# A trunk layer's input projection: 4096 of its columns by Strassen's seven products, with transposed gates applied late

## The chip, the cores and the metric

One Trainium2 chip; the kernel is one launch on one of its cores. The metric is the device time of that launch in microseconds, lower is better. Of three runs the median is 2184.79 us (2183.13 to 2187.67). A core has five engines that work beside each other and wait for one another through semaphores: TensorE (PE; matrix multiplication, with its weight loads shown as PEld), VectorE (DVE), ScalarE (ACT), GpSimd (POOL) and SyncE (SP, which here only issues DMAs).

## The reference

One layer of a hybrid decoder: 1024 rows of 2048 values. One projection of the normalized input gives 7184 columns, which feed three mixers side by side; their output is normalized per head, gated, projected back and added to the input. Then the rows attend to 256 memory rows, and a final norm follows.

```python
h = rmsnorm(x, norm_mix[l])
(sb_q, sb_k, sb_v, sb_g,                     # stick-breaking attention: 4 x 1024 columns, 8 heads of 128
 gla_q, gla_k, gla_v, gla_r, gla_g,          # gated linear attention (GLA): 256, 256, 512, 16, 512
 sgu_u, sgu_v, sgu_g) = jnp.split(h @ w_in[l], IN_OFFSETS, axis=-1)   # spatial gating (SGU): 3 x 512
o_sb = from_heads(stick_breaking_attention(sb_q, sb_k, sb_v))
o_gla = from_heads(gla_chunked(gla_q, gla_k, gla_v, log_alpha))
o_sgu = chunked_sgu(jax.nn.gelu(sgu_u), jax.nn.gelu(sgu_v), sgu_norm[l], w_sgu[l], b_sgu[l])
mix = jnp.concatenate([o_sb, o_gla, o_sgu], axis=-1)
mix = rmsnorm(mix.reshape(B, S, N_MIX_HEADS, HEAD_DIM), out_norm[l]...).reshape(B, S, MIX_WIDTH)
gate = jax.nn.silu(jnp.concatenate([sb_g, gla_g, sgu_g], axis=-1))
x = x + (mix * gate) @ w_out[l]
x = x + memory_cross_attention(rmsnorm(x, norm_xattn[l]), rmsnorm(mem, norm_mem[l]), w_xq[l], w_xkv[l], w_xo[l])
return rmsnorm(x, final_norm)
```

## The kernel before, in words

**Arithmetic.** Each float32 operand of a large product is held as two float32r tiles that add up to it: `split_to` (L142) casts on ACT and subtracts on DVE. A product is three matmuls (`mm3`, L184): high x low, high x high, low x high. The normalized and transposed input `hT` lies in SBUF as sixteen such pairs of [128, 512] pieces for each half of the rows.

**Stages.** After the norm and the first columns of v (to about 115 us), `natural` (L269) computes blocks of 512 columns with rows on partitions: the rest of v, GLA's v, SGU's u and v, and the gates of SGU and GLA with their SiLU (to about 630 us); they go to scratch in DRAM. After the keys and values of the memory (to 700 us) comes the stretch that the change rewrites: `weave` (L224) runs a list of groups, each a weight load (`raw_weights`, a DMA by SP; `split_to`) and four *steps*. `column_block` (L195) is 128 columns in sixteen steps of six 128x512 matmuls, the columns on partitions. Between the steps stand *tasks*, each with a time counted in steps: SGU (a task `sgu_out` writes its result), then GLA in two pairs of heads, then the eight heads of attention. So projection matmuls fill the time in which the tasks wait for ACT and DVE. The gates of attention (`block_g`) lie beside SGU and GLA, k and q of head h+1 (`block_k`, `block_q`) beside head h; a head has 32 steps.

**GLA.** A pair of heads runs seven *levels* (a chunk of 128 rows, halved again and again). A level forms decay factors `d` (L653), scaled queries `ql` (L663) and keys (`d<-d,k`, L666) on DVE, multiplies them on PE (`z<-ql,d`) and copies the wanted blocks into `attn` under a mask (COPY_PREDICATED, L677). Its output `og` and SGU's `y` are multiplied by their gates on POOL (L749, L543) and go to `mix_scr`, transposed.

**Attention.** `attend` (L835): `scores` makes a tile of scores on PE, three activations, a DVE step (L861), a mask multiply on the diagonal (L863), a scan from the right (L865), a subtraction (L871) and an activation (L872). `turn`, 5.3 steps later, transposes two of those on PE and splits the result into `aTh` and `aTl`; `values` multiplies with v into the PSUM bank `av`, of which there is one. At the end of a quarter of the rows `square` copies the output out of PSUM (`oc`, L903) and squares it on ACT; `close`, 2.5 steps later, sums the squares with two matmuls by `ones_r` into the other half of the same bank, takes ln and exp on ACT (L914, L915) and multiplies `oc` (L917).

**Output projection.** `mixed` (L956) loads 128 columns of the mix for half of the rows and splits them; for k < 8 (attention) it also loads the gate, takes its SiLU and multiplies on POOL (L970). The order is k = 8 to 15 first.

**What sets the order.** PE runs the woven part in program order (`keep_in_program_order`, L172 to L182). The other engines' orders come from a scheduler that sees the dependences and the buffers. Each engine takes its instructions in order, so one that waits holds up all behind it. Buffers limit what can run ahead: three raw weight tiles (`wr`), three split ones (`wh`, `wl`), four PSUM banks for projections (`pj`), two for scores (`z`), one for transposes (`tr`), one `av`.

```python
def split_to(hi, lo, src, eng=dve):
    act.copy(hi, src)
    eng.tensor_tensor(out=lo, in0=src, in1=f32(hi), op=ALU.subtract)
...
UNIT, LAG_T, STEP_T, LAG_V, LAG_S, AHEAD = 32 / 12, 5.3, 2, 2, 2.5, 4
```

## Time and profile before

| | value |
|---|---|
| median of three runs | 2184.79 us (2183.13 to 2187.67) |
| the profiled execution: its own time, the span of the profile | 2184.6 us |
| PE, PEld busy | 2125.8 us (97%), 1767.4 us (81%) |
| DVE, ACT, POOL busy | 1020.7 (47%), 860.9 (39%), 163.5 us (7%) |
| matmul records | 10525 |
| DMA | 231.18 MB, 106 GB/s on average |

The profile gives each engine's busy time; a view by stretches gives it for a window of the span, with the instruction count in brackets; a view by groups gives, for each line, engine, operation and shape, the count, the busy time, the mean of one in ns, the idle time of the engine just ahead of them and what ended it. The order in time lists start, duration and instruction. A line number is that of the kernel before unless said otherwise.

### The profile page before, as it was taken

To read this page: it belongs to the slowest core of one execution; us is meant where nothing else is said; L and a number is where in the kernel's file an instruction comes from. 1 tells how busy PE (TensorE), PEld (TensorE's weight loads), DVE (VectorE), ACT (ScalarE), POOL (GpSimd) and SP (SyncE) were. 2 spreads that over 40 slices of the span, in tenths; PEclk is the share of its full clock that TensorE was granted. 3 is DMA by queue.
4 is the path that set the end of the run, shared out by engine and by line. 5 is a ranking of instruction groups with operands and counts; after the bars stand their busy time and mean duration, and the time that the engine had idled before them with its cause. 6 is when DMAs were issued, how large, how long until landed. Compare 5 with 4: busy or idle time off the path is not lost.

```text
span 2184.6 us, 28465 instructions
## 1 busy us (share of the span) xinstructions
PE 2125.8 (97%) x10525; PEld 1767.4 (81%) x10525; DVE 1020.7 (47%) x1984; ACT 860.9 (39%) x1987; POOL 163.5 (7%) x273
## 2 busy tenths in 40 slices
PE   6999999999999999999999999999989999999997
PEld 6998888888887767878888888888877878888885
DVE  6621211111115627375377677776753121377674
ACT  6421111221215424242356565666654121356552
POOL 2110000000000110101111111111012000000001
PEclk9999999999999999999999999999999999999999
DMA  7541321331317621313222222222267231655632
GB/s 215 151 146 49 126 87 49 97 97 49 98 55 219 184 61 44 107 34 92 78 57 55 56 63 56 61 54 56 83 192 231 69 124 49 207 201 154 216 121 92
DMA packets 181847, 231.18 MB, mean 106 GB/s; under 512 B 17270, under 2 KB 106956, under 8 KB 179532
## 3 DMA queue, kind: packets, MB, share of 16 engines
q1 hardware_dynamic: 170572, 214.68, 32.1%
q0 software_dynamic: 11136, 14.69, 2.6%
q8 instruction: 83, 1.36, 0.3%
q14 instruction: 56, 0.46, 0.1%
HBM read 177.93 MB, written 51.38 MB: 105 GB/s over the span
## 4 chain that ended last, share of the span: by engine, by line
PE 44%; DVE 8%; ACT 5%; issue 4%; DMA 2%; POOL 1%; DVEq 0%; SPq 0%; POOLq 0%; ACTq 0%
PE pj L175 31%; PE z L175 6%; PE av L175 4%; PE tr L180 1%; DVE a L865 1%; DVE a L871 1%; PE tr L175 1%; ACT a L872 1%; DMA mraw<-mix 1%; ACT t L859 1%; ACT t L860 1%; DVE t L861 1%; DVE ql L663 1%; ACT t L858 1%; DVE wl L144 1%
## 5 line engine op out<-in xcount | busy, mean ns | idle before, releaser
L144 DVE TENSOR_TENSOR wl<-wr,wh 128x512 fp32r<-128x512 f32 (+1 forms) x392 | 267.6, 683 | 773.8 <-ACT wh L143 767.6
L175 PE MATMUL pj<-slot,wh 128*128 128x512 f32 x2048 | 576.9, 398 | 1.6 <-DVE qT L144 1.6
L143 ACT CAST wh<-wr 128x512 fp32r<-128x512 f32 (+1 forms) x395 | 237.6, 602 | 798.4 <-PE av L175 548.6
L175 PE MATMUL pj<-wh,slot 128*128 128x512 f32 (+1 forms) x1760 | 500.7, 370 | 0.0
L175 PEld LDWEIGHTS pj<-slot,wh 128*128 128x128 f32 x2048 | 369.7, 188 | 72.4 <-issue 2.3
L175 PEld LDWEIGHTS pj<-wh,slot 128*128 128x128 f32 x1760 | 321.5, 190 | 54.8
L175 PE MATMUL pj<-wl,slot 128*128 128x512 f32 (+1 forms) x880 | 328.9, 374 | 1.7 <-DVE wl L144 1.5
L175 PE MATMUL pj<-slot,wl 128*128 128x512 f32 x1024 | 327.9, 391 | 0.0
L175 PEld LDWEIGHTS pj<-slot,wl 128*128 128x128 f32 x1024 | 192.2, 188 | 42.7
L175 PEld LDWEIGHTS pj<-wl,slot 128*128 128x128 f32 x880 | 167.1, 190 | 30.3 <-DVE wl L144 2.3
L175 PE MATMUL z<-wh,slot 128*128 128x512 f32 x576 | 178.6, 390 | 0.7 <-DVE slot L144 0.7
L175 PEld LDWEIGHTS z<-wh,slot 128*128 128x128 f32 x576 | 108.2, 188 | 24.1 <-DVE slot L144 1.9
L175 PE MATMUL z<-wl,slot 128*128 128x512 f32 x288 | 112.5, 391 | 4.4 <-DVE xo L982 2.7
L861 DVE SCALAR_TENSOR_TENSOR t<-z,t 128x384 f32<-128x384 f32 (+2 forms) x96 | 53.4, 556 | 94.3 <-ACT t L860 94.2
L872 ACT ACTIVATE a<-a 128x384 f32<-128x384 f32 (+2 forms) x96 | 50.4, 525 | 114.5 <-DVE a L871 114.4
L175 PE MATMUL pj<-slot,oT 128*128 128x512 f32 x384 | 92.7, 396 | 0.0
L175 PE MATMUL tr<-wh,slot 128*128 128x512 f32 x288 | 88.7, 389 | 0.0
L175 PE MATMUL av<-wh,slot 128*128 128x512 f32 x288 | 88.7, 389 | 0.0
L175 PEld LDWEIGHTS pj<-slot,oT 128*128 128x128 f32 x384 | 71.0, 188 | 15.7
L175 PE MATMUL z<-kT,qT 128*128 128x512 f32 (+3 forms) x288 | 71.1, 355 | 0.0
L175 PEld LDWEIGHTS z<-wl,slot 128*128 128x128 f32 x288 | 54.0, 188 | 17.2 <-DVE xo L982 3.6
L144 DVE TENSOR_TENSOR aTl<-tr,aTh 128x512 fp32r<-128x512 f32 (+2 forms) x112 | 55.2, 493 | 19.3 <-ACT aTh L143 18.2
(252 smaller groups left out, 2684.2 us busy)
## 6 DMA issues: line engine op xcount, KB each, us to landing
wr<-in_w_in_dram SPq DMA_DIRECT2D x216, 256.0 KB, 2.8
wr<-in_w_out_dram SPq DMA_DIRECT2D x88, 256.0 KB, 2.8
xt<-in_x_dram SPq DMA_DIRECT2D x32, 256.0 KB, 4.8
wr<-in_w_xkv_dram SPq DMA_DIRECT2D x32, 256.0 KB, 3.2
v<-v_scr POOLq DMA_DIRECT2D x64, 128.0 KB, 2.8
xr<-in_x_dram SPq DMA_DIRECT2D x32, 256.0 KB, 5.1
x<-xo SPq DMA_DIRECT2D x32, 256.0 KB, 4.4
x2t<-x SPq DMA_DIRECT2D x8, 1024.0 KB, 7.2
```

Of the source, the lines that this page charges most:

```text
L143: act.copy(hi, src)
L144: eng.tensor_tensor(out=lo, in0=src, in1=f32(hi), op=ALU.subtract)
L175: i = pe.matmul(o, l, r, start=start, stop=stop)
L180: i = pe.transpose(o, i_, ident)
L663: dve.tensor_tensor(out=gl["ql"][r_, :, hh, :].rearrange("p c (b i) -> p c b i", i=h), in0=gl["q"][r_, :].rearrange("p (c b i) -> p c b i" ...
L858: act.activation(tw, z, AF.Abs)
L859: act.activation(tw, tw, AF.Exp, scale=-1.0)
L860: act.activation(tw, tw, AF.Ln, bias=1.0)
L861: dve.scalar_tensor_tensor(out=tw, in0=z, scalar=0.0, in1=tw, op0=ALU.max, op1=ALU.add)
L865: dve.tensor_tensor_scan(out=aw[:, ::-1], data0=tw[:, ::-1], data1=tw[:, ::-1], initial=init, op0=ALU.add, op1=ALU.max)
L871: dve.tensor_tensor(out=aw, in0=z, in1=aw, op=ALU.subtract)
L872: act.activation(aw, aw, AF.Exp)
```

## The change

**Seven products for eight.** Two blocks of 128 columns, two halves of the 2048 input values and two halves of the 1024 rows make a 2x2 by 2x2 product of blocks. Strassen's scheme replaces its eight block products by seven, on sums and differences of the blocks; four sums of products then give the result. This is done for 4096 columns: q and k of attention (a pair is a head's q and k), its gate, and the gates of GLA and SGU, which were `natural` blocks. Sixteen pairs, in two passes over all of them:

- The **first pass** computes products 1, 7 and 6 beside SGU and GLA: per pair eight *units* of nine matmuls, which count as 1.5 steps. Per unit two DMAs load a raw tile of [128, 512] with the four weight blocks, POOL adds two overlapping parts of it (`combine_first`, 384 elements a partition), and the sum is split. `evac_first` copies product 1 on ACT, adds it to the two others on DVE and writes both to DRAM (`part_scr`).
- The **second pass** computes products 5, 2, 3 and 4 beside attention: units of twelve matmuls, which count as 2; the POOL subtraction (`combine_second`, 2 x 128 elements) works in place. `evac_second` copies two products on ACT, subtracts on POOL from the two parts read back, and has four DVE additions from PSUM; the results go to DRAM: q and k to `qk_scr`, gates to `g_scr`. For four of the pairs (gates of GLA and SGU) it also takes the SiLU there: exp, ln, exp on ACT and a POOL multiply for each of four tiles, in buffers `se` of the raw weights' pool.

**The sums of the input.** `sums_round`, eight times, adds the two parts of four pieces of `hT` on POOL, forms five sums on DVE and writes seven tiles to DRAM; `place` reads them back for each pass and splits them (56 in all). The GLA q and k blocks move ahead of everything (steps 0 to 64), their results to DRAM; the first pass is steps 64 to 256, the second 256 to 512.

**What follows.** Attention reads q and k back from DRAM and splits them (`load_k`, `load_q`); a head has 30.3 steps. The mask multiply on DVE becomes an `affine_select` on POOL. `square` only squares; `close` sums with one float32 matmul, and its last DVE operation reads the output from PSUM. SGU and GLA no longer apply their gates; `mixed` does for k >= 8, with two loads into the raw weights' pool and a POOL multiply. `actp` has twelve buffers and a second pool `more` four, `wr` four. On PE 128x512 matmuls become 384 fewer and the two of `close` one; with no rows merged, SP's order has 1441 rows for 811, POOL's 669 instructions for 273, DVE's 2145 for 1986, ACT's 2026 for 1781.

```diff
-        def square(o, sh):
-            sq = sb.tile([P, 256], F32, tag="sq", name="sq")
-            t = sb.tile([P, 2, 256], F32R, tag="sh", name="sh")
-            oc = sb.tile([P, 256], F32, tag="oc", name="oc")
-            dve.tensor_copy(oc, o[0][:, :256])
             act.activation(sq, o[0][:, :256], AF.Square)
-            dve.tensor_copy(t[:, 0, :], sq)
-            dve.tensor_tensor(out=t[:, 1, :], in0=sq, in1=f32(t[:, 0, :]), op=ALU.subtract)
-            sh += [sq, t, oc]
+            sh.append(sq)
 
         def close(p, o, sh):
-            sq, t, oc = sh
-            st = o[0][:, 256:]
-            for i in range(2):
-                mm(st, ones_r, t[:, i, :], i == 0, i == 1)
+            sq, st = sh[0], o[0][:, 256:]
+            mm(st, ones_f, sq, True, True)
             act.activation(sq, st, AF.Ln, scale=1.0 / P, bias=eps_t[:, 0:1])
             act.activation(sq, sq, AF.Exp, scale=-0.5)
-            on = sb.tile([P, 256], F32, tag="on", name="on")
-            dve.scalar_tensor_tensor(out=on, in0=oc, scalar=col("out", h), in1=sq, op0=ALU.mult, op1=ALU.mult)
-            sp.dma_start(on_scr[h][:, p * 256:p * 256 + 256], on)
+            dve.scalar_tensor_tensor(out=sq, in0=o[0][:, :256], scalar=col("out", h), in1=sq, op0=ALU.mult, op1=ALU.mult)
+            sp.dma_start(on_scr[h][:, p * 256:p * 256 + 256], sq)
...
+    AHEAD_RAW = 2
+    def quarters(pairs, joint=0):
+        raw, tw = {}, {}
+        units = [[(pair, k, banks) for k in range(8)] for pair in pairs for banks in ({},)]
...
+        def load(j):
+            for i in range(0 if not j else j + AHEAD_RAW, min(j + AHEAD_RAW + 1, len(units))):
+                fetch(i)
+            pair, k, _ = units[j]
...
+            t, n = pair["combine"](raw.pop(j))
+            hi = whl.tile([P, 512], F32R, tag="wh", name="wh")
+            lo = whl.tile([P, 512], F32R, tag="wl", name="wl")
+            split_to(hi[:, :n], lo[:, :n], t[:, :n])
...
+            for i, c in pair["products"]:
+                th, tl = cut((hi, lo), c * P, c * P + P)
+                sh, sl = pair["sums"].at(i, k)
+                mm(banks[i], th, sh, k == 0, False)
+                mm(banks[i], th, sl, False, False)
+                mm(banks[i], tl, sh, False, k == 7)
...
+    def combine_first(raw):
+        t = bp.tile([P, 3 * P], F32, tag="ts", name="ts")
+        pool.tensor_tensor(out=t, in0=raw[:, :3 * P], in1=raw[:, P:], op=ALU.add)
+        return t, 3 * P
+
+    def combine_second(raw):
+        r3 = raw.rearrange("p (b n) -> p b n", n=P)
+        pool.tensor_tensor(out=r3[:, 0:4:3], in0=r3[:, 0:4:3], in1=r3[:, 2:0:-1], op=ALU.subtract)
+        return raw, 4 * P
...
+            act.copy(c12, banks[5])
+            act.copy(c21, banks[2])
+            pool.tensor_tensor(out=c11, in0=c11, in1=c12, op=ALU.subtract)
+            pool.tensor_tensor(out=c22, in0=c22, in1=c21, op=ALU.subtract)
+            dve.tensor_tensor(out=c12, in0=banks[3], in1=c12, op=ALU.add)
...
+            for t, b, half in ((c12, 1, 0), (c22, 1, 1), (c21, 0, 1), (c11, 0, 0)):
+                if silu:
+                    e = wraw.tile([P, 512], F32, tag="wr", name="se")
+                    act.activation(e, t, AF.Exp, scale=-1.0)
+                    act.activation(e, e, AF.Ln, bias=1.0)
+                    act.activation(e, e, AF.Exp, scale=-1.0)
+                    pool.tensor_tensor(out=t, in0=t, in1=e, op=ALU.mult)
...
         if k >= 8:
-            t = wraw.tile([P, 512], F32, tag="wr", name="mraw")
+            t, g_ = (wraw.tile([P, 512], F32, tag="wr", name=nm) for nm in ("mraw", "graw"))
             sp.dma_start(t, mix_scr[k - 8][:, sl])
+            sp.dma_start(g_, g_scr[k][:, sl])
+            pool.tensor_tensor(out=t, in0=t, in1=g_, op=ALU.mult)
```

How the change moves instructions is shown at three places. The first is PE at the end of a quarter in the attention, before (`av<-sh,ones_r` is the sum of squares, `av<-aTl,v` the next quarter's first values, `pj` the projection):

```order
L175 MATMUL pj<-slot,wh 128x512 x4
L175 MATMUL pj<-slot,wl 128x512 x2
L175 MATMUL av<-sh,ones_r 128x256 x2
L175 MATMUL pj<-slot,wh 128x512 x4
L175 MATMUL pj<-slot,wl 128x512 x2
L175 MATMUL av<-aTl,v 128x256
L175 MATMUL av<-aTh,v 128x256 x2
```

The same place of the change (`av<-sq,ones_f` is the sum of squares):

```order
L207 MATMUL pj<-slot,wh 128x512 x2
L207 MATMUL pj<-slot,wl 128x512
L207 MATMUL av<-sq,ones_f 128x256
L207 MATMUL av<-aTl,v 128x256
L207 MATMUL av<-aTh,v 128x256 x2
L207 MATMUL av<-aTl,v 128x256
L207 MATMUL av<-aTh,v 128x256 x2
L212 MATMUL tr<-ident,a 128x128 x3
```

The six projection matmuls between the sum and the next values are gone from this place. Of the 32 sums, 17 stand directly ahead of values now, seven have twelve matmuls between, and the last of each head has more.

The second place is DVE in the levels of GLA (`wl` is a split of projection weights; `d`, `ql`, `attn` are the level's), before:

```order
L677 COPY_PREDICATED attn<-masks,z 128x8x64 x2
L663 TENSOR_TENSOR ql<-q,d 64x8x64 x2
L653 TENSOR_TENSOR d<-bc 128x1024
L666 TENSOR_TENSOR d<-d,k 128x1024
L677 COPY_PREDICATED attn<-masks,z 128x16x32 x2
L663 TENSOR_TENSOR ql<-q,d 64x8x64 x2
L144 TENSOR_TENSOR wl<-wr,wh 128x512
L666 TENSOR_TENSOR d<-d,k 128x1024
L653 TENSOR_TENSOR d<-bc 128x1024
L677 COPY_PREDICATED attn<-masks,z 128x32x16 x2
```

And of the change (`ts` is what POOL has added):

```order
L877 COPY_PREDICATED attn<-masks,z 128x8x64 x2
L863 TENSOR_TENSOR ql<-q,d 64x8x64 x2
L853 TENSOR_TENSOR d<-bc 128x1024
L866 TENSOR_TENSOR d<-d,k 128x1024
L176 TENSOR_TENSOR wl<-ts,wh 128x384 x2
L877 COPY_PREDICATED attn<-masks,z 128x16x32 x2
L863 TENSOR_TENSOR ql<-q,d 64x8x64 x2
L853 TENSOR_TENSOR d<-bc 128x1024
L866 TENSOR_TENSOR d<-d,k 128x1024
L176 TENSOR_TENSOR wl<-ts,wh 128x384 x2
```

Two splits of 384 stand in each level, each behind a POOL addition, where about one split of 512 stood in every second level.

The third is SP where the output projection starts (`mraw` is a tile of the mix, `graw` of the gate, `wr` a weight), before:

```order
L963 DMA mraw<-mix_161 128x512
L154 DMA wr<-in_w_out_dram 128x512
L963 DMA mraw<-mix_162 128x512
L154 DMA wr<-in_w_out_dram 128x512
L918 DMA on_152<-on 128x256
L963 DMA mraw<-mix_163 128x512
L154 DMA wr<-in_w_out_dram 128x512
```

And of the change:

```order
L186 DMA wr<-in_w_out_dram 128x512 x2
L1157 DMA mraw<-mix_263 128x512
L1158 DMA graw<-g_146 128x512
L1157 DMA mraw<-mix_264 128x512
L1158 DMA graw<-g_147 128x512
L1110 DMA on_137<-sq 128x256
L186 DMA wr<-in_w_out_dram 128x512
L1157 DMA mraw<-mix_265 128x512
L1158 DMA graw<-g_148 128x512
L186 DMA wr<-in_w_out_dram 128x512
```

A tile takes two loads in place of one, and both come from the pool of four buffers that the weights use too; a buffer comes free when POOL has multiplied (gate) or the split has read it (mix).

More of the change, by code (lines that the diff above doesn't have):

```diff
@@ L229, in weave @@
         groups[0][0]()
-        for j, (_, steps) in enumerate(groups):
+        for j, (_, steps, *w) in enumerate(groups):
             if j + 1 < len(groups):
@@ new lines, in trunk, with place, stage_load @@
+    summed = {}
+    sB, sA = Sums(), Sums()
+    def place(sums, i, r, pool=actp):
+        if r % 4 == 0:
+            sums.t[i, r // 4] = (slot(pool=pool), slot(pool=pool))
+        hi, lo = (t[:, r % 4, :] for t in sums.t[i, r // 4])
+        split_to(hi, lo, summed.pop((i, r)))
+    def stage_load(i, r, pool):
+        t = pool.tile([P, 512], F32, tag="st", name="st", bufs=6 if pool is cq else 10)
+        sp.dma_start(t, sum_scr[i, r])
+        summed[i, r] = t
+    pr0, pr1 = gla_blocks(0, range(4)), gla_blocks(1, (0, 2, 1, 3))
@@ new lines, in trunk, with to_cq @@
+    groups += pr0[0] + pr0[1] + [g for both in zip(*pr1) for g in both]
+    def to_cq():
+        kv.close()
+        bp.open()
+        cq_open()
+    later(3.2, to_cq)
+    for m in range(2):
+        later(2 + m, mem_keys, m)
+    for j in range(8):
+        later(5 + j, gla_rank, j // 4, 4 * (j % 4))
+    for r in range(8):
+        later(8 + 4.5 * r, sums_round, r)
+    for n, (r, i) in enumerate([(r, i) for r in range(8) for i in (1, 7, 6)]):
+        t = 48.2 + 0.7 * n if n < 12 else 64.2 + 0.8 * (n - 12)
+        later(max(46, t - 4), stage_load, i, r, cq)
+        later(t, place, sB, i, r)
@@ L512, in sgu_load @@
+    groups += quarters([first(n) for n in range(16)], 2)
+    later(UB + 0.01, more.close)
+    sta = Stage("sta", 10, "right")
     def sgu_load(s):
-        t = {nm: sg.tile([P, 512], F32, tag=f"in{nm}", name=nm) for nm in ("sv", "su", "sg")}
-        for nm in ("sv", "su", "sg"):
+        t = {nm: sg.tile([P, 512], F32, tag=f"in{nm}", name=nm) for nm in ("sv", "su")}
+        for nm in ("sv", "su"):
             sp.dma_start(t[nm], nat_scr[nm][s])
@@ L797, in trunk @@
+    for n, (i, r) in enumerate(late):
+        later(UA + 0.1 + 0.6 * (n - 6), stage_load, i, r, sta)
+        later(UA + 0.2 + 0.6 * n, place, sA, i, r)
+    groups += quarters([second(n) for n in range(16)])
     sb = Stage("sb")
     kTs, qTs = {}, {}
-    consts = {}
     def sb_open():
         sb.open()
-        before = sb.tile([P, P], F32, name="before")
-        pool.affine_select(out=before, in_=ones_f, pattern=[[-1, P]], compare_op=ALU.is_gt, fill=0.0,
-                           base=0, channel_multiplier=1)
-        consts["before"] = before
@@ L1116, in load_wxo @@
         if n == 0:
-            wxo[k] = [(slot(), slot())]
+            wxo[k] = [tuple(slot(pool=actp if k else more) for _ in range(2))]
         h, l = wxo[k][0]
@@ L1193, in trunk @@
     xa.close()
+    more.close()
     if dbg is not None:
```

322 lines of the change are left out of this document (207 added, 115 removed).

## The prediction

> **What bounds the kernel now.** First the page: the busy time of each engine, then the span in forty slices (digits are tenths of a slice).
>
> ```profile
> span 2184.6 us, 28465 instructions
> ...
> PE 2125.8 (97%) x10525; PEld 1767.4 (81%) x10525; DVE 1020.7 (47%) x1984; ACT 860.9 (39%) x1987; POOL 163.5 (7%) x273
> ...
> PE   6999999999999999999999999999989999999997
> ...
> DVE  6621211111115627375377677776753121377674
> ACT  6421111221215424242356565666654121356552
> ...
> PEclk9999999999999999999999999999999999999999
> ```
>
> TensorE is busy for 97% of the span, at full clock in every slice, and falls under nine tenths only at both ends and in slice 31. Of 2184.6 us it is idle for 58.8. So matmuls that go away shorten the span, as long as the other engines can follow. They are near half load on average, but not evenly: the next view gives the busy time of each engine, with the instruction count, in the stretches that the change touches (columns: stretch, its length, PE, PEld, DVE, ACT, POOL, granted clock, DMA share, GB/s).
>
> ```profile
> 300.00:600.00 300.00, 300.00 (x1326) 248.47 (x1325) 39.35 (x60) 57.95 (x95) 0.00 (x0) 1.00 0.27 82
> 700.00:800.00 100.00, 97.62 (x476) 75.73 (x476) 50.61 (x140) 35.70 (x138) 21.04 (x30) 1.00 0.52 148
> 900.00:1000.00 100.00, 96.00 (x483) 78.43 (x483) 65.91 (x98) 38.66 (x71) 8.69 (x7) 1.00 0.21 62
> 926.00:978.00 52.00, 51.06 (x249) 40.97 (x248) 35.34 (x47) 23.57 (x31) 1.97 (x1) 1.00 0.15 41
> 1110.00:1550.00 440.00, 436.67 (x2275) 365.17 (x2274) 310.20 (x602) 269.96 (x607) 51.74 (x134) 1.00 0.23 59
> 1600.00:1700.00 100.00, 93.49 (x400) 74.00 (x400) 40.84 (x58) 44.71 (x83) 21.22 (x16) 1.00 0.70 226
> ```
>
> The stretch 300 to 600 is pure projection: 300.0/1326 = 0.2262 us for a 128x512 matmul. In 700 to 800 (spatial gating) PE loses 2.4%, around the GLA levels (900 to 1000) 4.0%, in seven heads of attention (1110 to 1550, 62.9 us a head) 0.8%, where the output projection starts (1600 to 1700) 6.5%.
>
> **The change part by part.** The sum is made against the profiled execution, 2184.6 us, which is 0.2 below the median of the runs.
>
> *Matmuls.* 4096 columns took 3072 matmuls; 16 pairs x 8 units x 7 products x 3 take 2688. 384 x 0.2262 = **-86.9 us**. At the end of each quarter of a head one f32 matmul takes the place of two f32r ones (32 times); each f32 matmul leaves two records.
>
> ```profile
> L175 PE MATMUL av<-sh,ones_r 128*128 128x256 f32 x64 | 13.6, 289 | 1.9 <-DVE sh L905 1.3 <-DVE sh L906 0.5
> L175 PE MATMUL av<-state,q 128*128 128x256 f32 x28 | 8.3, 378 | 0.0
> L175 PE MATMUL z<-ql,d 128*128 128x128 f32 x224 | 28.2, 279 | 7.2 <-DVE d L666 6.9
> ```
>
> The old pair costs 13.6/32 = 0.425 us, an f32 matmul of this size 8.3/14 = 0.59: +5.4. PE's own term is **-81.5 us**.
>
> *What the other engines get.* Each of 256 units now has an addition on POOL ahead of its split (ACT cast, DVE subtract).
>
> ```profile
> L144 DVE TENSOR_TENSOR wl<-wr,wh 128x512 fp32r<-128x512 f32 x360 | 254.1, 706 | 746.4 <-ACT wh L143 740.2 <-DMA xr<-in_x_dram 4.8 <-PE tr L180 0.6
> L143 ACT CAST wh<-wr 128x512 fp32r<-128x512 f32 x363 | 224.6, 619 | 766.9 <-PE av L175 548.6 <-PE pj L175 185.3 <-DMA wr<-in_w_xkv_dram 9.5
> L970 POOL TENSOR_TENSOR mraw<-mraw,graw 128x512 f32<-128x512 f32 x16 | 21.2, 1326 | 57.0 <-ACT graw L969 57.0
> L749 POOL TENSOR_TENSOR og<-og,gg 128x256 f32<-128x256 f32 x16 | 13.4, 841 | 102.8 <-ACT v L748 102.8
> L871 DVE TENSOR_TENSOR a<-z,a 128x384 f32<-128x384 f32 x16 | 8.8, 552 | 2.3 <-POOL carry L869 2.3
> ```
>
> The second pass's POOL addition is of 256 elements a partition: 0.84 us. The first pass's is of 384, which has no row: midway between 0.84 and 1.33, 1.08. A 384-wide DVE operation takes 0.55, a 512-wide one 0.69 to 0.71.
>
> These durations hold apart from each other only. The order in time of DVE and POOL shows what happens when they meet (start, duration, instruction):
>
> ```profile
> 719.23 0.69 DVE L542 TENSOR_TENSOR y<-y,rs_r 128x512 f32<-128x512 f32 x1
> ...
> 720.50 1.77 DVE L144 TENSOR_TENSOR wl<-wr,wh 128x512 fp32r<-128x512 f32 x1
> ...
> 726.37 1.87 DVE L524 SCALAR_TENSOR_TENSOR sv<-sv,rs_r,gn 128x512 f32<-128x512 f32 x1
> ```
> ```profile
> 720.06 1.66 POOL L543 TENSOR_TENSOR y<-y,sg 128x512 f32<-128x512 f32 x1 [570.56 <-ACT wh L143]
> 726.40 1.29 POOL L543 TENSOR_TENSOR y<-y,sg 128x512 f32<-128x512 f32 x1 [4.68 <-issue]
> ```
>
> A DVE operation on two SBUF inputs that meets a POOL addition ends 0.55 us after it (720.50+1.77 against 720.06+1.66) and has taken 1.77 instead of 0.69. So I count POOL's additions as DVE time too, for the share that meets such operations. [...]
>
> *First pass.* The stretch 926 to 978 holds the seven levels of a GLA pair: 7 x 28.2/14 = 14 us of PE's time for the levels, 38 for projection, so 38/(9 x 0.2262) = 18.7 units. DVE: 35.3, less 7 old splits (4.8), plus 18.7 x 0.55 = 10.3: 40.8. POOL: 18.7 x 1.08 = 20.2. Without meeting, DVE has 40.8 of 52 and nothing is lost; if all of POOL's time falls on DVE it has 61 of 52, 9 us over. More than half of DVE's work here reads two SBUF tiles, so I take half: 51 of 52, with 4 us lost a stretch. Two stretches 8, the spatial gating half as much (its window is lighter, and the old POOL multiplies there go away): **+12** (0 to 28).
>
> *Second pass beside attention.* A head lasts 62.9 - 1.7 x 6 x 0.2262 + 0.7 = 61.3 us for PE (30.3 steps for 32). The groups of instructions that go from DVE:
>
> ```profile
> L863 DVE TENSOR_TENSOR t<-t,before 128x128 f32<-128x128 f32 x64 | 18.5, 289 | 1.7
> L906 DVE TENSOR_TENSOR sh<-sq,sh 128x256 fp32r<-128x256 f32 x32 | 13.5, 421 | 0.7
> L903 DVE COPY oc<-av 128x256 f32<-128x256 f32 x32 | 13.1, 409 | 0.0
> L905 DVE CAST sh<-sq 128x256 fp32r<-128x256 f32 x32 | 9.9, 310 | 3.7 <-ACT sq L904 3.7
> ```
>
> The same view, of the stretch 1110 to 1550 alone, for one row of DVE and one of ACT:
>
> ```profile
> L865 DVE TENSOR_TENSOR_SCAN a<-t,carry 128x512 f32<-128x512 f32 x27 | 34.6, 1281 | 0.5
> ```
> ```profile
> L860 ACT ACTIVATE t<-t 128x512 f32<-128x512 f32 x41 | 25.9, 632 | 0.9
> ```
>
> DVE: 310.2/7 = 44.3, less these four groups (55.0/8 = 6.9), plus 7.15 more splits (4.9), plus 1.89 evacuations of four additions (5.2): 47.5. ACT: 270.0/7 = 38.6, plus 7.15 x 0.62 and 1.89 x 2 copies of 0.6: 45.3. POOL: 15.15 x 0.84 + 1.89 x 2 x 1.33 = 17.7 of additions, 29% of the head. About 21 two-input DVE operations a head (15.15 splits, two of k, four of q) meet one with that chance and then wait some 1.0 us (half an addition and the 0.55): +6, so DVE has 53.5 of 61.3. No stretch of before is that dense; the nearest lost 4.0% (900 to 1000) and 0.8% (this one). The 4.0% would be 3.2% of 61.3 more, 2.0 us a head; the wait of the next paragraph gives DVE time to catch up, so I take half, for 8 heads **+8** (0 to 30; 30 is 47.5+17.7 = 65.2 against 61.3, with all of POOL's time on DVE).
>
> *A new wait at the end of a quarter.* The sums of squares stand in the one PSUM bank `av`, beside the quarter's output, and the next quarter's values go into the same bank. In order of time, all engines:
>
> ```profile
> 1174.79 0.40 PE L175 MATMUL av<-sh,ones_r 128*128 128x256 f32 x2
> ...
> 1175.97 0.46 ACT L914 ACTIVATE sq<-av,eps_t 128x256 f32<-128x256 f32 x1
> ...
> 1176.47 0.42 ACT L915 ACTIVATE sq<-sq 128x256 f32<-128x256 f32 x1
> 1176.49 0.19 PEld L175 LDWEIGHTS av<-aTl,v 128*128 128x128 f32 x1 [0.35 <-ACT sq L914]
> ...
> 1176.92 0.48 DVE L917 SCALAR_TENSOR_TENSOR on<-oc,cols,sq 128x256 f32<-128x256 f32 x1
> ```
>
> The bank is free today when L914 has read it; PE ran the six projection matmuls that its order has there and lost 0.35 us. The change drops the copy `oc`, so the bank stays taken until the last multiplication (L917's place) has read the output too: 0.42 and 0.48 longer. And PE's order now puts the next values directly behind the sum in 17 of the 32 quarters, with no matmul between (12 in seven others). There PE waits for 0.47+0.42+0.47 = 1.4 us at least; with the queues ahead of ACT and DVE as they were here (1175.19 to 1175.97, and 1176.89 to 1176.92) 2.2. I take 1.8: 17 x 1.8 = **+31** (22 to 53; the upper end is 17 x 2.7, should DVE's queue, fuller now, add half a microsecond, and one us in each of the seven). What stands behind the waiting matmul is all of PE's work.
>
> *Gates in the evacuation.* Four evacuations of the second pass also put twelve 512-wide activations into ACT's queue, 12 x 0.63 = 7.6 us, ahead of the activations of the scores and the cast of the transposed weights, which PE waits for. The turn comes 5.3 steps (7.2 us) after the scores, whose chain takes some 5.2 (four activations of 0.63, two DVE operations of 0.69, a scan of 1.28): 2.0 are spare and up to 5.6 are lost each time. The attention's activations can stand among the twelve, since the scheduler mixes them; I take some 2 us: 4 x 2 = **+8** (0 to 22).
>
> *Start of the output projection.* Sixteen tiles now need two loads and a POOL multiplication, in buffers shared with the weights.
>
> ```profile
> L963 SPq DMA_DIRECT2D mraw<-mix x16: 319/320/388, 1547.6 to 1626.9; - x16
> ...
> DMA to landing us min/median/max: 2.5/3.2/6.5
> ```
>
> The order has the next load wait for the previous multiplication's buffer: 3.2 + 1.33 = 4.5 us a tile, against 12 x 0.2262 = 2.7 of PE's work for it. 16 x 1.8 = 29. The last head's matmuls and projection units stand between the first tiles, and part of the 6.5 us that this stretch loses is the same idle time: **+12** (8 to 30). Gone in return: sixteen POOL multiplies of GLA (13.4 us), eight of spatial gating, off the path already.
>
> *Sums.* A round has four POOL additions (5.3 us) and five on DVE (3.5), which exclude each other: 8.8 x 8 = 70 us of some 76 between step 8 and the first pass. Another 56 tiles are split (0.71 on DVE, 0.62 on ACT). Both lie beside projections that leave DVE light (300 to 600: 13%): **+3** (0 to 15).
>
> *Loads.* SP issues 1441 rows for 811, at 0.32 us (the row above) some 200 us more of an engine that only issues.
>
> ```profile
> wr<-in_w_in_dram SPq DMA_DIRECT2D x216, 256.0 KB, 2.8
> ```
>
> A weight lands in 2.8 us and is asked for two units ahead (2 x 2.7 in the second pass, 2 x 2.0 in the first); the DMA share beside attention is 0.23, so twice the bytes fit. I put nothing for it; if a store that waits holds up the loads behind it in SP's queue, that cover is gone, and a unit can be late by up to 2.8. The ranges above stand for that.
>
> Sum: -81.5 + 12 + 8 + 31 + 8 + 12 + 3 = -7.5, hence **2177 us**; the ends of the terms give 2133 (30 of costs) and 2281 (178).
>
> **The rivals.**
> *A, all but the bank hidden.* POOL's additions fall beside DVE operations that read PSUM, and the buffers carry the rest. For it: DVE and ACT stay under 78% of a head. Against it: the 4% already lost around the GLA levels. -81.5 + 22 + 8: 2133.
> [...]
> *C, scans meet POOL as well.* Twelve scans a head, one for each tile of scores: 12 x 0.29 x 1.0 = 3.5 us a head more, 57 of 61.3, and the loss in the attention triples: 16 on the forecast, 2193. For it: a scan names two SBUF inputs. Against it: they are one tile, and no row shows it. [...]
> *D, the bank's wait is at its upper end.* 53 for 31: 2199. For it: ACT's queue grows by 17% and DVE's by POOL; against it: while PE waits no new work comes to them.
> *No change.* The costs come to 77 to 86.
> That the change does not remove the matmuls is no rival: their count follows from the order.
>
> **How the numbers follow.** Forecast (2160 to 2180) 0.32; A 0.18; no change (within 0.2%, about what a measurement of this kernel can tell) 0.10; B 0.20; C 0.10; D 0.10. Faster is the forecast and A, 0.50; slower B, C and D, 0.40. The forecast's own range is 2160 to 2180; the one asked for, 2125 to 2245, leaves out a part of A and the upper half of B's spread, under 0.2 together.
>
> **What would show it.** Right: projection matmuls down by 384 at 0.226 us, PE busy near 2044; the first values of a quarter waiting 1.4 to 2.7 us for the DVE multiplication that replaces L917, 17 times; in the GLA levels 4 us lost a stretch. Wrong towards A: the attention stretch at 97% PE with no idle time but those 17. [...] A PE busy time that does not fall by about 80 would break the first term, a bank freed before that multiplication the fourth.

## The result, and the profile after

The changed kernel takes 2367.48 us (median of four runs, 2365.24 to 2372.35) against 2185.51 us before: a ratio of 1.0838, 95% interval 1.0823 to 1.0854. It is 8.4% slower, where 2177 us, a little faster, was forecast; the time lies above the whole range.

The page of the profile after, busy times and slices of the span:

```profile
span 2363.4 us, 30403 instructions
...
PE 2134.0 (90%) x10141; PEld 1752.6 (74%) x10141; DVE 1211.4 (51%) x2143; ACT 981.2 (42%) x2232; POOL 538.5 (23%) x664
...
PE   6999999999987899998787788888788999999997
...
PEclk9999999999998999999898989998999999999999
```

There are 384 matmul records fewer (10141 for 10525), as the change says. But PE is busy for 8 us *more*, not 81 less, and idle for 229 us in place of 59. The row PEclk has eights where there were none before. So two things were lost: time in which PE had nothing to do, and time in which it worked at less than full clock.

Views by stretch put numbers on both. The borders are the same events in both kernels: the first matmul of the spatial gating, the first and the last of the GLA levels, the first scores, the last values. Columns as before: length, PE, PEld, DVE, ACT, POOL busy, granted clock. First the kernel before:

```profile
0.00:715.00 715.00, 696.26 (x3472) 587.60 (x3472) 184.13 (x346) 191.70 (x398) 26.91 (x39) 1.00 0.37 111
715.00:832.00 117.00, 114.62 (x539) 87.64 (x538) 59.42 (x152) 44.19 (x147) 21.04 (x30) 1.00 0.39 109
832.00:995.00 163.00, 155.38 (x815) 128.66 (x814) 108.48 (x156) 55.60 (x102) 13.29 (x11) 1.00 0.22 63
995.00:1074.00 79.00, 79.00 (x388) 66.40 (x388) 27.71 (x64) 19.62 (x60) 12.39 (x19) 1.00 0.35 97
1074.00:1599.00 525.00, 518.98 (x2686) 433.95 (x2685) 367.25 (x705) 319.44 (x712) 57.91 (x150) 1.00 0.23 61
1599.00:2184.60 585.60, 561.59 (x2636) 463.19 (x2634) 273.67 (x563) 230.40 (x570) 31.99 (x24) 0.99 0.46 151
```

And after:

```profile
0.00:701.00 701.00, 666.18 (x3296) 556.50 (x3297) 242.25 (x418) 196.68 (x416) 99.70 (x99) 0.99 0.47 146
701.00:813.00 112.00, 88.71 (x376) 68.91 (x376) 71.29 (x172) 48.28 (x158) 44.62 (x53) 0.89 0.51 143
813.00:985.00 172.00, 155.58 (x792) 127.91 (x791) 134.63 (x200) 66.54 (x130) 66.20 (x56) 0.97 0.43 122
985.00:1094.00 109.00, 100.29 (x458) 79.84 (x457) 71.52 (x127) 49.10 (x115) 37.41 (x41) 0.98 0.66 209
1094.00:1778.00 684.00, 558.56 (x2604) 456.01 (x2605) 417.75 (x671) 391.87 (x848) 250.10 (x387) 0.91 0.41 118
1778.00:2363.40 585.40, 564.70 (x2622) 463.45 (x2621) 273.97 (x556) 228.78 (x568) 40.43 (x31) 0.98 0.47 154
```

Length less PE is idle time; length times what is missing from a clock of 1 is lost to the clock. The views round the clock to two places; the last column of the table below is worked out from the unrounded records.

| stretch | idle before, after | lost to the clock before, after |
|---|---|---|
| up to the spatial gating | 18.7, 34.8 | 1.7, 8.5 |
| spatial gating | 2.4, 23.3 | 0, 11.9 |
| GLA levels | 7.6, 16.4 | 0, 5.1 |
| to the first scores | 0, 8.7 | 0, 1.7 |
| attention (second pass) | 6.0, 125.4 | 1.7, 63.7 |
| after the last values | 24.0, 20.7 | 5.0, 9.4 |

PE is idle for 170.6 us more. Its busy time should have fallen by 81.5 us and rose by 8.2, which is 89.7 too much. The clock's records account for 74 of these: the changed kernel ran at half clock for 200.8 us, PE was busy in 154.0 of them, and half of that, 77.0 us, was lost (3.3 before; the rest of the table's 100.4 us fell into waits). The other 16 us stay open. 170.6 + 8.2 are the 178.8 us between the spans. Two thirds of both losses lie in the attention. In that stretch the view of waits (what PE waited for, us in total, times, longest) has one row that outweighs the rest:

```profile
PE av L207 <- DVE sq L1109: 98.4, 23, 8.4
PE pj L207 <- DVE c L704: 11.0, 8, 3.0
PE av L207 <- DVE aTl L176: 9.2, 14, 1.9
```

The largest row of the same stretch before was the wait for the Ln:

```profile
PE av L175 <- ACT sq L914: 2.8, 6, 2.0
```

The 98.4 us are the wait for the bank `av`, of the same kind as forecast, but three times as long. The order in time at the longest shows where it comes from:

```profile
1338.70 0.60 PE L207 MATMUL av<-sq,ones_f 128*128 128x256 f32 x2
...
1340.53 0.46 ACT L1107 ACTIVATE sq<-av,eps_t 128x256 f32<-128x256 f32 x1
1340.89 0.62 ACT L711 ACTIVATE se<-se 128x512 f32<-128x512 f32 x1
...
1345.12 1.14 ACT L712 ACTIVATE se<-se 128x512 f32<-128x512 f32 x2
1346.16 0.62 ACT L710 ACTIVATE se<-c 128x512 f32<-128x512 f32 x1
1346.68 0.40 ACT L1108 ACTIVATE sq<-sq 128x256 f32<-128x256 f32 x1
...
1347.12 0.48 DVE L1109 SCALAR_TENSOR_TENSOR sq<-av,cols,sq 128x256 f32<-128x256 f32 x1 [2.08 <-ACT sq L1108]
...
1347.66 0.58 PE L207 MATMUL av<-aTl,v 128*128 128x256 f32 x1 [8.36 <-DVE sq L1109]
...
1349.60 1.31 PE L207 MATMUL z<-kT,qT 128*128 128x384 f32 x3
...
1351.99 1.05 PE L207 MATMUL pj<-slot,wh 128*128 128x512 f32 x2
1352.84 0.63 PE L207 MATMUL pj<-slot,wl 128*128 128x512 f32 x1
...
1353.89 0.40 PE L207 MATMUL pj<-slot,wl 128*128 128x512 f32 x1
```

The Exp (L1108) stands in ACT's order behind the SiLU of an evacuation, 5.7 us after the Ln, and the bank is held all the while. After the wait two 128x512 matmuls take 0.85 us from start to start (1351.99 to 1352.84), 0.43 each, where full clock gave 0.226; by 1353.89 the modelled duration of one is 0.40 again, for 0.63 at 1352.84. In another quarter it is DVE that holds the bank:

```profile
1562.65 2.18 POOL L701 TENSOR_TENSOR c<-c,c 128x512 f32<-128x512 f32 x1
...
1564.87 0.69 DVE L703 TENSOR_TENSOR c<-pj,c 128x512 f32<-128x512 f32 x1 [1.09 <-POOL c L701]
1565.47 0.68 DVE L1071 TENSOR_TENSOR a<-z,a 128x512 f32<-128x512 f32 x1
1566.09 0.69 DVE L704 TENSOR_TENSOR c<-pj,c 128x512 f32<-128x512 f32 x1
...
1567.30 0.68 DVE L706 TENSOR_TENSOR c<-pj,c 128x512 f32<-128x512 f32 x1
1567.89 0.47 DVE L1109 SCALAR_TENSOR_TENSOR sq<-av,cols,sq 128x256 f32<-128x256 f32 x1
...
1568.42 0.58 PE L207 MATMUL av<-aTl,v 128*128 128x256 f32 x1 [7.31 <-DVE sq L1109]
```

There the evacuation's additions stand ahead of the last multiplication, and the first of them waits for a POOL subtraction. Over the 32 quarters the mean time from the sum's end to the Ln's start is 1.26 us (0.45 before), between Ln and Exp 0.38 (0.18), between Exp and the multiplication 1.24 (0.62): 4.25 us until the bank is free, where the Ln freed it after 0.92 before.

### The profile page after: what moved, and what is told of

The parts are those of the page before. It is cut to its first block, busy times and chain, and to the rows that moved or that the text cites. A ratio compares the mean times of both kernels' runs of the same rounds, so it can differ in the third digit from the quotient of the medians.

```text
span 2363.4 us, 30403 instructions
## 1 busy us (share of the span) xinstructions
PE 2134.0 (90%) x10141; PEld 1752.6 (74%) x10141; DVE 1211.4 (51%) x2143; ACT 981.2 (42%) x2232; POOL 538.5 (23%) x664
## 5 line engine op out<-in xcount | busy, mean ns | idle before, releaser
L207 PE MATMUL pj<-slot,wh 128*128 128x512 f32 x2256 | 736.6, 413 | 27.5 <-DVE c L704 9.9
L207 PEld LDWEIGHTS pj<-slot,wh 128*128 128x128 f32 x2256 | 431.0, 198 | 129.4 <-DVE c L704 14.1
L207 PE MATMUL pj<-slot,wl 128*128 128x512 f32 x1128 | 445.4, 404 | 5.6 <-DVE wl L176 5.6
L207 PE MATMUL pj<-wh,slot 128*128 128x512 f32 (+1 forms) x1504 | 425.1, 369 | 0.0
L207 PEld LDWEIGHTS pj<-wh,slot 128*128 128x128 f32 x1504 | 274.1, 191 | 47.4
L672 POOL TENSOR_TENSOR ts<-raw 128x384 f32<-128x384 f32 x128 | 144.0, 1129 | 264.1 <-DVE wl L176 188.2
L677 POOL TENSOR_TENSOR wr<-wr 128x256 f32<-128x256 f32 x128 | 107.5, 842 | 197.6 <-DMA wr<-in_w_in_dram 144.4
L207 PE MATMUL av<-aTl,v 128*128 128x256 f32 (+1 forms) x160 | 53.2, 332 | 108.5 <-DVE sq L1109 98.4
L175 ACT CAST wh<-ts 128x384 fp32r<-128x384 f32 x128 | 65.2, 510 | 148.8 <-PE pj L207 131.2
L176 DVE TENSOR_TENSOR wl<-ts,wh 128x384 fp32r<-128x384 f32 x128 | 77.0, 610 | 77.1 <-ACT wh L175 76.9
```

The lines of the kernel that those rows point to most:

```text
L207: i = pe.matmul(o, l, r, start=start, stop=stop)
L672: pool.tensor_tensor(out=t, in0=raw[:, :3 * P], in1=raw[:, P:], op=ALU.add)
L677: pool.tensor_tensor(out=r3[:, 0:4:3], in0=r3[:, 0:4:3], in1=r3[:, 2:0:-1], op=ALU.subtract)
```

## The experiments

Each ran once, beside a run of the kernel before on the same chip (2183.4 for the first four, 2186.8 for the next four, 2187.3 for the last). "Attention" is the stretch from the first scores to the last values; its idle time and lost clock are worked out as above, from unrounded records. The kernel before differs by up to 3.9 us between these runs, so a difference of a few microseconds says nothing.

**e1_own_copy**: the output leaves the bank early.

```diff
             act.activation(sq, o[0][:, :256], AF.Square)
-            sh.append(sq)
+            oc = sb.tile([P, 256], mybir.dt.bfloat16, tag="oc", name="oc")
+            dve.tensor_copy(oc, o[0][:, :256])
+            sh += [sq, oc]
...
-            dve.scalar_tensor_tensor(out=sq, in0=o[0][:, :256], ...)
+            dve.scalar_tensor_tensor(out=sq, in0=oc, ...)
```

> The changed kernel, but the output of a quarter is copied out of the PSUM bank av again as in the kernel before (one DVE copy a quarter), so that the bank comes free after the Ln; the copy is in bfloat16, which alters the attention's output, and the pool of small tiles has three buffers for four. Theory 'bank': the values of the next quarter waited 98 us for the last multiplication (DVE sq L1109), and waits over 3.4 us let the clock fall to half, so both go: idle time of PE in the second pass 122 us down to some 35, its granted clock from 0.91 to 0.97 or more, the whole 2367 down to about 2230 (2205 to 2255). Rival 'load': DVE, ACT and POOL cannot follow in the second pass and the same wait comes back at other places: above 2310.

Measured: 2329 us. That is the rival's side. The wait for the multiplication is gone, but the view of waits has others at the same matmuls:

```profile
PE av L207 <- DVE aTl L176: 28.0, 26, 5.3
PE av L207 <- ACT sq L1109: 25.1, 17, 3.6
PE av L207 <- ACT sq L1103: 18.5, 10, 3.5
```

(L1109 is the Ln here, L1103 the square.) With nothing between the sum and the next values in PE's order, PE waits for the Ln itself, 1.5 us each. So the long hold of the bank explains 38 us (less what the added copy costs), and the missing matmuls make a wait of whatever comes next. On the theory's 3.4 us: in the changed kernel half clock came within 3.4 us after 19 of the 20 idle stretches of PE that were longer than that, but also after 7 of the 8 of 2.5 to 3.4 us.

**e2_gap**: work between the sum and the values.

```diff
-                    tasks.append((t + LAG_V, lambda ...: values(p, m, d, o, f, l)))
+                    later_by = 1.5 if first else 0
+                    tasks.append((t + LAG_V + later_by, lambda ...: values(p, m, d, o, f, l)))
...
-            t += LAG_V - STEP_T + 0.01
+            t += LAG_V - STEP_T + 0.01 + (1.5 if p == 0 else 0)
```

> The changed kernel with the first values of a quarter 1.5 steps later, so that a unit of at least twelve matmuls (2.7 us) stands in PE's order between the sum of squares and the next values everywhere; nothing else is altered. Theory 'bank': 17 places get 2.7 us of work each, 46 us of idle time go, most waits fall under 3.4 us and with them the half clock: about 2280 (2250 to 2305). Rival 'load': the values wait as long after the unit as before it: above 2340.

Measured: 2311 us, 6 above the "bank" theory's range and 29 below the rival's. The wait for the multiplication falls from 98 to 21.9 us; but others grow:

```profile
PE av L207 <- DVE sq L1109: 21.9, 13, 3.4
PE pj L207 <- DVE c L704: 21.2, 13, 3.4
PE av L207 <- DVE aTl L176: 11.7, 11, 2.5
PE tr L212 <- DVE aTl L176: 9.6, 5, 5.3
```

**e3_close_alone**: the new end of a quarter in the kernel before.

```diff
-            oc = sb.tile([P, 256], F32, tag="oc", name="oc")
-            dve.tensor_copy(oc, o[0][:, :256])
...
-            for i in range(2):
-                mm(st, ones_r, t[:, i, :], i == 0, i == 1)
+            mm(st, ones_f, sq, True, True)
...
-            dve.scalar_tensor_tensor(out=on, in0=oc, ...)
+            dve.scalar_tensor_tensor(out=sq, in0=o[0][:, :256], ...)
```

> The kernel before with the new end of a quarter alone (square without copies, one float32 matmul, the last multiplication reads PSUM). PE's order there keeps six matmuls between the sum and the next values. Theory 'bank': some 24 quarters wait about 1 us more (0.9 later release), waits stay under 3.4 us and the clock stays full: 2185 + 5 + 15 to 25 = 2205 to 2215. Rival: the new end is harmless where ACT and DVE are not full: 2183 to 2195.

Measured: 2203 us, 19.6 above the kernel before on the same chip: a loss of the theory's kind, 2 us below its range. The page's waits:

```profile
PE av L175 <- DVE sq L909: 19.8, 24, 3.3
```

24 quarters wait, as counted, and the granted clock stays at 0.996. So the new end is a loss by itself, of 20 us: in the attention PE is idle for 15 us more and busy for 6 more. It takes the new order and the fuller queues to make 98 of it.

**e4_filler**: useless matmuls in the waits.

```diff
             mm(st, ones_f, sq, True, True)
+            if closed[0] in FILLED:
+                b = bank("tr")
+                for n in range(12):
+                    mm(b[:, :P], ones_f, ones_f, True, True)
+            closed[0] += 1
```

> The changed kernel with twelve matmuls of 128x128 float32 that nobody reads (some 3 us of PE, in the bank tr) behind the sum of squares in the 17 quarters where nothing stood between it and the next values: PE does more, and the wait for the bank ends no earlier. Theory 'clock': the time lost after a wait is the half clock, which filled waits avoid; waits longer than 3 us keep up to 3 us of true idle, so most half-clock windows of the second pass go: 61 us of lost clock there down to 15 to 30, the whole 2367 down to 2325 (2310 to 2345). Rival 'no clock effect': the time stays within 2360 to 2385, or rises by the filler.

Measured: 2357 us, 10.7 us *less* than the changed kernel with 204 matmuls more (8.5 less than the fastest of its four runs), but short of the gain that was expected. The stretch of the attention:

```profile
1095.00:1767.00 672.00, 584.10 (x3015) 482.27 (x3016) 418.71 (x672) 391.58 (x848) 249.49 (x387) 0.96 0.42 120
```

Idle time goes from 125 to 88 us, by the fillers; PE busy 559 to 584 us, though the fillers alone are 17 x 12 x 0.25 = 51 us (0.25 from the 128x128 float32 matmuls of the GLA levels). So the other matmuls took 26 us less, at a clock of 0.96 for 0.91, and the lost clock falls from 64 to 27 us. The clock effect is there, of the expected size; the whole time that was expected forgot that the filler also takes PE's time where the wait was shorter, and that it holds up the next transposition (PE waited 16.9 us for the bank `tr`).

**e5_gap_and_copy**: the diffs of e1 and e2 together.

> The changed kernel with both: the copy of the output (e1_own_copy) and the first values 1.5 steps later (e2_gap). e1 gave 2329, e2 2311. Theory 'order and bank add up': e2's remaining waits for the last multiplication (22 us, some of them near 3.4 us) go and with them a part of its 37 us of lost clock in the second pass: 2285 (2270 to 2298). Rival 'the wait moves': the waits for the split of the transposed weights (DVE aTl) and for the evacuation (DVE c) grow by as much: 2305 to 2315.

Measured: 2309 us: the rival. The two do not add; the waits for `aTl` and the evacuation take over:

```profile
PE pj L207 <- DVE c L704: 23.0, 14, 3.6
PE av L207 <- DVE aTl L176: 21.7, 22, 3.9
```

The attention still loses 80 us idle and 32 us of clock, so the bank's release is not all that is wrong there.

**e6_no_combining**: no POOL operation ahead of the splits.

```diff
-        pool.tensor_tensor(out=t, in0=raw[:, :3 * P], in1=raw[:, P:], op=ALU.add)
-        return t, 3 * P
+        return raw, 3 * P
...
-        pool.tensor_tensor(out=r3[:, 0:4:3], in0=r3[:, 0:4:3], in1=r3[:, 2:0:-1], op=ALU.subtract)
```

> The changed kernel without the POOL operations ahead of the splits in both passes (256 of them, 251 us of POOL): raw blocks are split as they come, so the projected q, k and gates are not the reference's, and q is scaled by a further 1/1000. [...]

Measured: 2318 us, 50 less. The stretch of the attention:

```profile
1067.00:1727.00 660.00, 553.87 (x2603) 452.99 (x2604) 405.04 (x671) 392.73 (x846) 154.53 (x271) 0.92 0.42 122
```

The gain is spread: 24 us in the attention (660 for 684), 9 each in spatial gating and GLA, 9 in the stretches before and between. The wait for the bank stays (90.3 us, 23 times). So POOL's additions cost more than the 25 us by which the splits of 512 and the scans are longer in the changed kernel than before (266.4 for 254.1 and 106.0 for 93.7 us).

**e7_gating_apart**: the tiles of the spatial gating further apart.

```diff
-    SG, NV, MX, OU, SP = 88, 2.1, 4.8, 9.2, 3.2
+    SG, NV, MX, OU, SP = 88, 2.1, 4.8, 9.2, 3.7
```

> The changed kernel with the spatial gating's tiles 3.7 steps apart for 3.2, as in the kernel before; the linear attention follows 3.5 steps later. In the changed kernel PE is idle for 24 us of the gating's 119 and at 0.89 clock. Theory 'too dense': its chain gets 0.7 us more a tile, and half of the six waits of 2 to 3 us for the normalized v go, with half of the 13 us of lost clock: 2350 (2340 to 2360). Rival 'the chain is late by its queue, not by its spacing': 2360 to 2372.

Measured: 2371.5 us: the rival. The waits for the normalized v fall from 14.2 to 8.3 us, and the stretch of the GLA levels behind them is 8 us longer.

**e8_raw_gates**: no SiLU in the evacuation.

```diff
-        src, to, silu = PAIRS[n]
-        st = {}
+        src, to, _ = PAIRS[n]
+        silu, st = False, {}
```

> The changed kernel without the SiLU in the second pass's evacuation (48 activations of 0.62 us and 16 POOL multiplications left out, so the gates of k >= 8 are applied raw). Theory 'bank': the four long waits that held the Exp behind these activations (5.8, 6.4, 8.4 and 5.8 us) shrink to about 3.5, 12 us, and with them some 8 us of lost clock: 2345 (2335 to 2357). Rival 'load on ACT': attention as a whole runs better, below 2325.

Measured: 2350.5 us, 17 less, within the "bank" theory's range. The attention is 21 us shorter: 18 us of idle time and 3 of busy time. The wait for the bank falls by as much, from 98.4 to 80.7 us.

**e9_fine_steps**: tasks may stand between the products of a unit.

```diff
-        return [(lambda j=j: load(j), [lambda j=j: step(j)], units[j][0]["weight"]) for j in range(len(units))]
+        return [(lambda j=j: load(j), [lambda j=j, s=s: step(j, s) for s in range(len(units[j][0]["products"]))], 0.5)
+                for j in range(len(units))]
...
-        for f, half, t in ((load_k, 1, -5), (load_q, 1, -4), (load_k, 0, 0), (load_q, 0, 12)):
+        for f, half, t in ((load_k, 1, -3.95), (load_q, 1, -3.9), (load_k, 0, 0), (load_q, 0, 12)):
```

> The changed kernel with a unit cut into steps of one product (three matmuls, half a step) in both passes, so that tasks can stand between the products of a unit; the loads of k and q for a head's second half come one step later. In the changed kernel a task can only stand at every second step (12 matmuls, 2.7 us), so tasks gather at the same place and the distance from scores to their transposition is 2 or 3 units (5.4 or 8.1 us) for a chain of some 5.2. Theory 'coarse units': the 17 places without a matmul get three, the chains get 1 to 2 us more: 2320 (2290 to 2345). Rival 'load': 2355 or more.

Measured: 2347 us, 2 above the theory's range and 8 below the rival's.

**e10_fine_gap_copy**: the diffs of e1, e2 and e9 together.

> e5_gap_and_copy (2309) with the fine steps of e9_fine_steps. Theory 'coarse units': what e5 still lost in the attention (80 us idle, 32 us of lost clock, against 6 and 2 in the kernel before) falls by a third: 2270 (2240 to 2290). Rival 'load': 2300 to 2312.

Measured: 2293 us, 16.5 less than e5, again less than expected; the order in fine steps is worth some 17 to 20 us either way. The largest wait is now the evacuation's:

```profile
PE pj L207 <- DVE c L706: 25.3, 13, 3.7
...
PE pj L207 <- DVE c L708: 12.6, 10, 4.2
```

**e11_fine_gap_copy_evac**: the evacuation's subtractions on DVE.

```diff
-            pool.tensor_tensor(out=c11, in0=c11, in1=c12, op=ALU.subtract)
-            pool.tensor_tensor(out=c22, in0=c22, in1=c21, op=ALU.subtract)
+            dve.tensor_tensor(out=c11, in0=c11, in1=banks[5], op=ALU.subtract)
+            dve.tensor_tensor(out=c22, in0=c22, in1=banks[2], op=ALU.subtract)
```

> e10_fine_gap_copy, with the two subtractions of the second pass's evacuation on DVE straight from PSUM in place of POOL, so that the four banks come free without POOL (the four products take all four projection banks; PE waited 23 us in e5 for DVE c L704, which waits for POOL). Theory 'banks': 12 us less than e10 (5 to 20). Rival 'DVE is as full': within 4 us of e10.

Measured: 2273 us, 19.4 less than e10, as the "banks" theory said. The waits for the evacuation fall from 38 to 17 us:

```profile
PE pj L207 <- DVE c L708: 8.6, 10, 2.3
PE pj L207 <- DVE c L706: 8.1, 8, 2.7
```

The four products of a unit hold all four projection banks, so PE cannot begin the next pair before the evacuation; in the kernel before a block held two of four.

**e12_floor**: e10 with the diffs of e6 and e8.

> e10_fine_gap_copy without the POOL combinations ahead of the splits and without the SiLU in the evacuation (projected values, gates and outputs are not the reference's; q scaled by a further 1/1000): what is left are the seven products, the evacuations' sums and the order. Theory 'added work': order, bank, combinations and SiLU together are the attention's loss, which falls under 30 us: 2190 (2170 to 2215). Rival 'something else bounds the second pass' (the loads on SP's queue, the shortage of projection banks): above 2235.

Measured: 2199 us, within the "added work" range. The attention loses 37 us idle and 8.5 us of clock:

```profile
1053.00:1611.00 558.00, 520.50 (x2620) 428.73 (x2621) 415.73 (x703) 356.65 (x801) 140.38 (x255) 0.98 0.50 144
```

The rival, for which it had to stay above 2235, did not come true. Of e12's remaining waits the evacuation's are the largest again (27 us). But the saved matmuls do not come back as time. PE is busy there for 520.5 us against 519.0 before, with 70 projection matmuls fewer (1502 for 1572, 15.8 us at 0.226); half clock while it was busy is 7.8 us of it. Ahead of the first scores, 288 records fewer make that part only 20 us shorter (1053.4 for 1073.7). Where the rest goes was not tried.

The staircase, whole time: 2367 as changed; 2309 with the order and the bank mended; 2293 in fine steps; from there 2273 with the evacuation off POOL, or 2199 without combinations and SiLU. None of these is faster than the kernel before.

## Why the prediction was wrong

1. **Matmuls, -81.5 us: the count right, the time not.** There are 384 records fewer. PE's busy time, which was to fall to near 2044 us, came to 2134.0; with the time lost to half clock taken out it fell by 65 us (2122.5 to 2057.0). The forecast took PE to stay at full clock and fed; it was idle for 170.6 us more, and at half clock for 200.8.
2. **The bank, +31 (22 to 53): right mechanism and place, wrong size.** 98.4 us in 23 waits: 81 of them at the 17 places, 4.8 each where 1.8 were taken, and 17 at the seven others. The step that failed is "with the queues ahead of ACT and DVE as they were here 2.2; I take 1.8": the queues were read from one quarter of the kernel *before* (over its 32 quarters the mean from the sum to the end of the multiplication is 2.6 us already), though the change puts evacuations and SiLU into those queues at the same times. The prediction had priced those additions by themselves, as if PE waited for one or the other; they stand in one chain. Against rival D it was said that no new work comes to ACT and DVE while PE waits; at 1338.70 the SiLU of an evacuation already stood in ACT's order. e3 shows the price with the old queues: 20 us. e8 shows that SiLU lengthens the waits.
3. **No term for the clock: 74 us by its records.** This is the largest single omission. The kernel before had no wait that mattered for the clock (it lost 3.3 us to it), its row PEclk said 9 everywhere, and the sum took each microsecond of waiting as one microsecond. e4 shows that it is more: work that nobody needs, put into the waits, shortens the run by 10.7 us.
4. **The attention's density, +8 (0 to 30): too low.** With order and bank mended the attention still loses 80 us idle (e5). The prediction took a loss rate from the densest row of before, 4%, and halved it. Two mechanisms were missed: tasks can only stand every 2.7 us (fine steps: 17 to 20 us), and the four products take all four banks (the evacuation off POOL: 19 us). Both could be read from the change: steps of weight 2, and four tags `pj` for four buffers.
5. **POOL's additions beside DVE: longer operations, and a price above the 23 that were taken.** Splits of 512 went from 706 to 741 ns, the scan from 1281 to 1387:

```profile
L176 DVE TENSOR_TENSOR wl<-wr,wh 128x512 fp32r<-128x512 f32 x360 | 266.4, 741 | 540.3 <-ACT wh L175 532.7 <-PE tr L212 1.8 <-DMA wr<-k 1.8
L1065 DVE TENSOR_TENSOR_SCAN a<-t,carry 128x512 f32<-128x512 f32 x32 | 44.4, 1387 | 0.8
```

   The order in time of the changed kernel gives the cause: of its 48 scans of 512, the 18 that overlap an operation on two tensors on POOL took 1.54 us on average, the 29 that overlap nothing on POOL 1.26; the evacuation's additions (L703), with one input in PSUM, take 0.69 although all 16 overlap such an operation. So scans do meet POOL, as rival C had it. But a meeting costs less than the 1.0 us that was taken: the 63 splits of 512 that overlap such an operation took 0.99 us, the undisturbed 0.69. POOL's addition at 726.40 shows no loss from its meeting: 1.29 us, no longer than its 1.33 apart (the 1.66 at 720.06 is longer). DVE is 61% busy in the attention (417.75 of 684) and did not become the bound. POOL's additions still cost 50 us (e6), where 23 were taken for the terms of both passes and the sums; e6 takes away the meetings and POOL's step ahead of each split together, so how much is due to which stays open.
6. **SiLU, +8 (0 to 22): right within its bounds**, 17 by e8.
7. **First pass and sums, +12 (0 to 28) and +3 (0 to 15): too low.** By the table the spatial gating lost 21 us idle and 12 of clock more, the levels 9 and 5, the rest of the first pass 9 and 2, the stages ahead of it 16 and about 7: some 80 in all (less what the clock lost while PE waited). For the gating only the spacing was tried (e7: no gain); without POOL's additions the first pass is some 22 us shorter (e6). What delays its chain beyond that stays open. In the rounds of sums, where the additions on POOL and DVE were taken to exclude each other, the 8 of the 40 DVE additions that overlap one on POOL took 1.24 us on average, the other 32 0.69.
8. **The output projection, +12 (8 to 30): too high.** From the last values to the end it took 585.4 us against 585.6. The tiles' loads lie mostly beside the last head, in the attention's stretch; by the view of these tiles PE waited for them for 4.1 us in all, 2.3 before.
9. **Loads, put at nothing: small at most.** By the view of waits PE waited for the split of projection weights for 9.0 us in all, 2.3 before; how much of it the loads caused is not shown.

## What to carry to other kernels

Price a new wait with the queues that the change will have, not with those of the profile: what the change adds to ACT and DVE stands in the same chain as the wait (in the longest, the Exp came 5.7 us after the Ln). In this kernel, which held TensorE at 97%, waits of several microseconds cost more than their length: half clock came after 19 of the 20 of over 3.4 us, and that and the waits lost three times what 384 fewer matmuls were to save. When interleaved work is cut into larger units, check how many places for tasks are left and how many buffers a unit takes.

## What the runs showed of the hardware

The granted clock has two values in the records of both kernels, 1 and 0.5, and changes at multiples of 3.413 us. With the span between the first and the last matmul cut into that grid, 45 pieces of the changed kernel had PE idle for more than half of the piece, and 41 of them were followed by half clock in the next; of 578 with PE idle for under a fifth, 3 were. In the kernel before only two pieces had PE idle for more than half, and half clock followed both. So no piece that is idle throughout was needed: 23 of the 45 were idle for 50 to 80%, and half clock followed 20 of these. By single idle stretches between matmuls, half clock came within 3.4 us after 19 of 20 of over 3.4 us, 7 of 8 of 2.5 to 3.4, 7 of 12 of 1.7 to 2.5 and 3 of 17 of 1.0 to 1.7. In the spatial gating, where PE is idle for 23.3 of 112 us, the granted clock is 0.89.

Useless matmuls shortened a run here (e4): 51 us of added work gave 10.7 us less time than the changed kernel's median.
